# Decay blocks of a Mamba-2 branch: difference and bound moved from VectorE to 16 ScalarE activations a group, with two smaller moves

## The chip, the cores and the metric

The kernel runs on one core of a Trainium2 chip. The core has five engines that each work through their own list of instructions in order and wait for one another by semaphores: TensorE (PE, matrix products and transposes, with its weight loads shown apart as PEld), VectorE (DVE), ScalarE (ACT), GpSimd (POOL) and SyncE (SP, which here only starts DMA transfers). The metric is the device time of one execution in microseconds (us).

## The reference

Two layers, each a feed-forward block, a mixer and a second feed-forward block, on 256 positions of width 1024; a norm at the end. All arithmetic is float32. The mixer runs two branches side by side on the same normed input, a Mamba-2 state-space branch (SSD: 32 heads of 64 in 4 groups, chunks of 128 positions, so two chunks) and a gated DeltaNet branch (8 heads). The change lies in the SSD branch, in the matrix called `decay`:

```python
log_a = (dt * a).reshape(b, nc, L, G, hg)
a_cum = jnp.cumsum(log_a, axis=2)
causal = jnp.tril(jnp.ones((L, L), dtype=bool))[None, None, :, :, None, None]
seg = a_cum[:, :, :, None] - a_cum[:, :, None, :]
decay = jnp.where(causal, jnp.exp(jnp.where(causal, seg, 0.0)), 0.0)
cb = jnp.einsum("bclgn,bcsgn->bclsg", Cc, Bc)
y_diag = jnp.einsum("bclsg,bclsgh,bcsghp->bclghp", cb, decay, xdt)
```

For each head and chunk this is a 128x128 block: the exponential of the difference of two running sums, where the row is not before the column. `a` is negative, so the difference is at most zero there; where the row is before the column it may be positive, and the kernel bounds it at zero and lets the product with a masked `cb` make it zero.

## The kernel before

**Products in three parts.** A float32 product is made of three products of rounded halves: each operand is split into a high part (`...h`, `whi`) and a low one (`...l`, `wlo`), and high x high, high x low and low x high are summed in one bank of PSUM (`mm3`). Nearly all of TensorE's work is such products.

**Weights.** They come as tiles of 128x1024 from memory, started by SyncE into a ring of five buffers (`wraw`). `prep` splits a tile: ScalarE copies it to `whi` (line 68) and VectorE subtracts to get `wlo` (line 71), in rings of five each. `take` hands the next tile to the products and prepares those that follow. So each tile costs ScalarE one copy and VectorE one subtraction, whatever else these engines do, and when either falls behind by five tiles, TensorE stands.

**The mixer's order.** A table of step names (`ORDER`) says in which order the steps of the two branches are written; the scheduler then sets the order of each engine's list from the dependences, its own estimates, and priorities. The steps around the change, in their order in time:

- `ssd_pre` (lines 1038 to 1054): for each of 4 groups two products of B and C into a bank of PSUM (`cbb`); VectorE masks them into `cbm` and ScalarE copies the part across chunks into `cbx` (both shown as `cbt`). Banks come from two pools of four, `trb` (short-lived) and `accb` (accumulators).
- `decay(g)` (lines 1059 to 1074) for group g: a DMA spreads the running sums of the group's 8 heads over all partitions (`dc`, 128x2048: 8 heads, 2 chunks, 128 positions); VectorE subtracts the column `ac` (2048 wide in one instruction) and bounds at zero; ScalarE takes the exponential; VectorE multiplies by `cbm`. Two buffers, one for groups 0 and 2 and one for 1 and 3.
- `xs_unit(g, i)`: two weight tiles through TensorE (`xs`) give 256 channels of the SSD's input; ScalarE makes the first product of a convolution of four taps (`ca<-xs,lp`), VectorE the other three (`ca<-xs,lp,ca`, of 255, 254 and 253 positions), and ScalarE applies silu into `xsT`. Exp and silu are in different tables of ScalarE, so the lists have an `ACT_TABLE_LOAD` before the first of each.
- `ssd(g)`: TensorE turns `xsT` (`xsb`, 8 transposes); VectorE makes `xD`, `xdt`, `xe`; TensorE multiplies by the decay block (`ydb`) and by the carried state (`yob`); VectorE adds them into `xD` and multiplies by the gate (`yz`); ScalarE squares and sums (`jk`), VectorE scales the sums (`sss`), GpSimd takes the power -1/2 (`srr`, line 210), and ScalarE scales `yz` by it (`yz<-yz,srr`).
- `gate`: tanh of two more tiles of columns (`t`, `tg`).
- `dn_T(hp)` and the DeltaNet branch's projection: TensorE turns a pair of heads (`oT`), VectorE gates it (`og`), ScalarE makes its high part (`bh`), VectorE its low part (`bl`), and TensorE multiplies both with a weight tile into four accumulators (`b`, lines 335 to 337). The SSD branch's projection follows later in the same way from `yz` (`yT`).
- at the mixer's end the gated sum of both is turned (`mT`) and split into `mh` (ScalarE) and `ml` (VectorE), and `close` multiplies it with the output weights (`o`): the first two tiles as one group, in `out_chunks`, for positions 0 to 127 (t = 0) and then 128 to 255.

Work of several steps is under way at once: while the SSD heads of group g run, the inputs of group g + 1 and the decay of group g + 2 are made.

Of the kernel before, what the change touches and what calls it, by code (L numbers as in the profile page):

```python
# [10 lines left out]
AF = mybir.ActivationFunctionType  # L11
ALU = mybir.AluOpType
# [4 lines left out]
P = 128  # L17
# [7 lines left out]
GS = 4  # L25
# [28 lines left out]
def trunk_kernel(ctx, tc, x, wst, wsm, norms, lpar, rpar, cst, out):  # L54
    nc = tc.nc
    V, A, G, PE = nc.vector, nc.scalar, nc.gpsimd, nc.tensor
# [10 lines left out]
    def act(o, i, func=AF.Copy, **kw):  # L67
        return A.activation(out=o, in_=i, func=func, **kw)  # L68

    def tt(o, a, b, op):  # L70
        return V.tensor_tensor(out=o, in0=a, in1=b, op=op)  # L71
# [4 lines left out]
    def ts(o, a, s1, op0, sc2=None, op1=None):  # L76
        if op1 is None:
            return V.tensor_scalar(out=o, in0=a, scalar1=s1, scalar2=None, op0=op0)
        return V.tensor_scalar(out=o, in0=a, scalar1=s1, scalar2=sc2, op0=op0, op1=op1)
# [7 lines left out]
    def trb(name):  # L87
        return trp.tile([P, 512], F32, tag="tr", name=name)

    def accb(name):  # L90
        return accp.tile([P, 512], F32, tag="acc", name=name)

    def small(shape, name, bufs=2):
        return sm.tile(shape, F32, tag=name, name=name, bufs=bufs)
# [54 lines left out]
    state = {"loaded": 0, "prepped": 0, "taken": 0, "last": None, "hold": False, "behind": {}, "late": {}, "first": 0, "turns": {}, "first_chunk": False, "cap": n_forms}  # L149
# [52 lines left out]
    def take():  # L202
        j = state["taken"]
        state["taken"] = j + 1
        ahead("loaded", limit[min(j + NSPL, n_forms) - 1], load)
        ahead("prepped", min(j + 1 if state["hold"] else j + NSPL, n_forms, state["cap"]), prep)
        return halves.pop(j)
# [11 lines left out]
    h = cpool.tile([P, 2, D], F32, name="h")  # L219
# [114 lines left out]
    def mm3(ps, lh, ll, rh, rl, start, stop):  # L334
        PE.matmul(ps, lh, rh, start=start, stop=False)  # L335
        PE.matmul(ps, lh, rl, start=False, stop=False)  # L336
        return PE.matmul(ps, ll, rh, start=False, stop=stop)  # L337
# [55 lines left out]
                        cut and a == 0 and kt == 1,  # L393
                    )

    def out_chunks(ps, stat, ks, last, group=1, split=False, first=None):

        for g0 in range(0, len(ks), group):
            kk = ks[g0 : g0 + group]
            ws = [(k, take()) for k in kk]  # L400
            for t in range(2):
                order = [(k, n) for n in range(2) for k in range(len(kk))]
                if t == 1 and not split:
                    m = len(kk) - 2 if len(kk) == NSPL else len(kk)
                    order = [(k, n) for k in range(m) for n in range(2)]
                    order += [(k, n) for n in range(2) for k in range(m, len(kk))]
                order = [(k, n, 0, 512) for k, n in order]
                if t == 1 and split:
                    order = [o for o in order if o[1] == 0]
                    order += [(k, 1, c, c + 256) for c in (0, 256) for k in range(len(kk))]  # L410
                state["sums"] = []
                for k, n, c0, c1 in order:
                    k, (wh, wl) = ws[k]
                    sh, sl = stat(k, t)
                    c = slice(n * 512 + c0, n * 512 + c1)
                    begin = k == 0 if first is None else first and t == n == 1
                    bank = ps[t][n][:, c0:c1]
                    if c0:
                        begin, bank = k == kk[0], ps[2][:, 0:256]
                    ins = mm3(bank, sh, sl, wh[:, c], wl[:, c], begin, k == last)  # L420
                    state["sums"].append(ins)

    def residual(po, nw):
        def add(t):
            banks = [(po[t][n][:], n * 512) for n in range(2)]
            if nw is None and t == 1:
                banks.append((po[2][:, 0:256], 768))
            for bank, c0 in banks:
                hv = h[:, t, c0 : c0 + bank.shape[-1]]
                ins = stt(hv, bank, 0.5, hv, ALU.mult, ALU.add)  # L430
            return ins

        if nw is None:
            return add
        norm_in(nw, add)

    def close(po, stat, n_k, nw):

        out_chunks(po, stat, list(range(2)), n_k - 1, group=2)
        out_chunks(po, stat, list(range(2, n_k - NSPL)), n_k - 1)  # L440
        state["hold"] = True
        out_chunks(po, stat, list(range(n_k - NSPL, n_k)), n_k - 1, group=NSPL, split=nw is None)
        return residual(po, nw)
# [149 lines left out]
    def mixer(l, nxt):  # L593
# [50 lines left out]
        ac = small([P, 2, 40], "ac", 1)  # L644
# [393 lines left out]
        def ssd_pre():  # L1038
            BT, CT = late["BC"][:, 0:4], late["BC"][:, 4:8]
            cbt = slots.tile([P, 3 * GS, P], F32, tag="sF", name="cbt")  # L1040
            late["cbx"] = cbx = cbt[:, 2 * GS :]
            late["cbm"] = cbm = cbt[:, : 2 * GS].rearrange("p (g t) l -> p g t l", g=GS)
            for g in range(GS):
                cbb = trb("cbb")
                PE.matmul(cbb[:, 0 : 2 * P], BT[:, g, 0:P], CT[:, g, :], start=True, stop=True)
                PE.matmul(cbb[:, 2 * P : 3 * P], BT[:, g, P : 2 * P], CT[:, g, P : 2 * P], start=True, stop=True)
                tt(
                    cbm[:, g],
                    cbb[:].rearrange("p (t o l) -> p t o l", t=2, o=2)[:, :, 0, :],
                    U[:, None, :].to_broadcast([P, 2, P]),  # L1050
                    ALU.mult,
                )
                act(cbx[:, g], cbb[:, P : 2 * P])
            yield
# [4 lines left out]
        def decay(g):  # L1059
            dc = slots.tile([P, 8, 2, P], F32, tag=("sA", "sB")[g % 2], name="dc")  # L1060
            nc.sync.dma_start(
                dc[:].rearrange("p h t l -> p (h t l)"),
                rdram[8 * g : 8 * g + 8].rearrange("a b -> (a b)").partition_broadcast(P),
            )
            tt(
                dc[:], dc[:],
                ac[:, :, 8 * g : 8 * g + 8].rearrange("p t h -> p h t")[:, :, :, None].to_broadcast([P, 8, 2, P]),
                ALU.subtract,
            )
            dv = dc[:].rearrange("p h t l -> p (h t l)")  # L1070
            ts(dv, dv, 0.0, ALU.min)
            act(dv, dv, AF.Exp)
            tt(dc[:], dc[:], late["cbm"][:, g, None].to_broadcast([P, 8, 2, P]), ALU.mult)
            decs[g] = dc

# [102 lines left out]
        def branch(kind, n, mk, tail=1):  # L1178
            ps = [[accb("b"), accb("b")] for _ in range(2)]
            held = {}  # L1180

            def stat(k, t):
                oh, ol = held[k // 2]
                return oh[:, k % 2, t * P : (t + 1) * P], ol[:, k % 2, t * P : (t + 1) * P]

            made = 1
            for j0 in list(range(n - tail)) + [n - tail]:
                js = range(j0, j0 + (tail if j0 == n - tail else 1))
                while made < min(js[-1] + 2, n):
                    mk(made)  # L1190
                    made += 1
                for j in js:
                    held[j] = brT.pop((kind, j))
                out_chunks(ps, stat, [2 * j + i for j in js for i in range(2)], 2 * n - 1, group=2 * len(js))
            return ps
# [57 lines left out]
        ps = branch("s", 8, ss_T)  # L1253
# [20 lines left out]
        po = [[accb("o"), accb("o")] for _ in range(2)]  # L1274

        def stat(k, t):
            return mh[:, k, t * P : (t + 1) * P], ml[:, k, t * P : (t + 1) * P]

        close(po, stat, 8, nxt)

    norm_first(nw0)
# [157 lines left out]
```

## Time and profile before

| | us |
|---|---|
| median of 3 runs | 1544.98 |
| lowest and highest of them | 1544.69, 1545.77 |
| the profiled execution | 1543.84 |
| its span in the trace | 1542.1 |
| granted clock of TensorE, mean | 0.999 |

The profile comes from one execution; its times are those of the trace, counted from the start of the span. Rows of groups give count, busy time, mean duration and the idle time of the engine just before them with what ended it. Rows of the timeline give start, duration, engine, line, operation, out<-in, shapes, a count where like instructions follow one another, and in brackets the idle time before and its releaser. All activations share line 68, VectorE's two-operand operations line 71, and its three-operand ones line 74, so rows are told apart by their tiles. The names are those of the program without numbers. What belongs to the mixers lies, in the first layer, between about 300 and 600 us, and in the second 762 us later.

### The profile page before, as it was taken

How to read it: one execution, taken by the hardware profiler on the slowest of the kernel's cores; microseconds unless marked ns; L12 is line 12 of the kernel's file. 1: busy time of each engine (PE TensorE's matmuls, PEld its weight loads, DVE VectorE, ACT ScalarE, POOL GpSimd, SP SyncE). 2: the span in 40 equal slices, each digit the busy share in tenths (PEclk: the TensorE clock that was granted, in tenths of full speed). 3: DMA queues.
4: the chain of work that ended last, by engine and by line, in shares of the span. 5: the costliest groups of instructions: out<-in, count | busy, mean ns of one | idle time of the engine just before them, and what ended most of it. 6: DMA issues, size and time to landing. Idle time of an engine off the chain costs nothing.

```text
span 1542.1 us, 29082 instructions
## 1 busy us (share of the span) xinstructions
PE 1525.1 (99%) x11473; PEld 1385.3 (90%) x11473; DVE 1229.8 (80%) x1859; ACT 949.8 (62%) x1536; POOL 82.6 (5%) x92
## 2 busy tenths in 40 slices
PE   8999999999999999999999999999999999999998
PEld 7999879999988888999899998899998888899997
DVE  5878768967899766789778887689579996678886
ACT  5656667766665645566555566776756666455565
POOL 0000010000000000000100012010000000000010
PEclk9999999999999999999999999999999999999999
DMA  7687765553565556577866687566346555556775
GB/s 272 187 266 227 232 223 174 183 164 112 180 209 172 157 174 191 184 252 217 264 221 227 204 254 238 182 196 186 117 137 204 180 167 187 175 179 191 250 241 156
DMA packets 98831, 305.73 MB, mean 198 GB/s; under 512 B 22837, under 2 KB 23813, under 8 KB 97670
## 3 DMA queue, kind: packets, MB, share of 16 engines
q1 hardware_dynamic: 93796, 290.95, 57.1%
q0 software_dynamic: 4608, 12.58, 5.0%
q8 instruction: 90, 1.47, 0.4%
q14 instruction: 47, 0.39, 0.1%
q10 hardware_dynamic: 290, 0.33, 0.1%
HBM read 297.72 MB, written 1.92 MB: 194 GB/s over the span
## 4 chain that ended last, share of the span: by engine, by line
PE 90%; DVE 3%; ACT 3%; DMA 2%; issue 1%; POOL 0%; SPq 0%; POOLq 0%; ACTq 0%; DVEq 0%
PE fc L346 10%; PE fc L340 9%; PE fc L345 9%; PE t L366 9%; PE o L337 4%; PE o L336 4%; PE o L335 4%; PE f L366 3%; PE b L337 3%; PE b L335 3%; PE b L336 3%; PE p L336 2%; PE p L335 2%; PE p L337 2%; PE xs L340 1%; PE xs L345 1%
## 5 line engine op out<-in xcount | busy, mean ns | idle before, releaser
L71 DVE TENSOR_TENSOR wlo<-wraw,whi 128x1024 fp32r<-128x1024 f32 x488 | 592.2, 1222 | 189.9 <-ACT whi L68 175.4
L68 ACT ACTIVATE whi<-wraw 128x1024 fp32r<-128x1024 f32 x488 | 511.4, 1059 | 266.8 <-PE fc L345 87.3
L346 PE MATMUL fc<-uW,wlo 128*128 128x256 f32 x1280 | 354.9, 277 | 0.0
L340 PE MATMUL fc<-uW,whi 128*128 128x256 f32 x1280 | 354.1, 277 | 0.0
L345 PE MATMUL fc<-uW,whi 128*128 128x256 f32 x1260 | 348.3, 276 | 0.0
L340 PEld LDWEIGHTS fc<-uW,whi 128*128 128x128 f32 x1280 | 240.5, 188 | 0.8
L346 PEld LDWEIGHTS fc<-uW,wlo 128*128 128x128 f32 x1280 | 240.5, 188 | 0.0
L345 PEld LDWEIGHTS fc<-uW,whi 128*128 128x128 f32 x1260 | 236.5, 188 | 0.8
L366 PE MATMUL t<-whi,uW 128*128 128x512 f32 x512 | 165.4, 397 | 0.0
L366 PEld LDWEIGHTS t<-whi,uW 128*128 128x128 f32 x512 | 95.9, 188 | 21.6 <-issue 1.3
L68 ACT ACTIVATE whi<-wsum 128x1024 fp32r<-128x1024 f32 x64 | 68.0, 1062 | 58.7 <-PE fc L345 32.3
L366 PE MATMUL t<-wlo,uW 128*128 128x512 f32 x256 | 100.1, 392 | 0.0
L71 DVE TENSOR_TENSOR wlo<-wsum,whi 128x1024 fp32r<-128x1024 f32 x64 | 78.2, 1222 | 8.3 <-ACT whi L68 5.9
L335 PE MATMUL b<-whi,bh 128*128 128x512 f32 x192 | 76.1, 398 | 0.3 <-ACT bh L68 0.2
L336 PE MATMUL b<-wlo,bh 128*128 128x512 f32 x192 | 75.0, 390 | 0.0
L337 PE MATMUL b<-whi,bl 128*128 128x512 f32 x192 | 74.3, 394 | 0.3 <-DVE bl L71 0.3
L340 PE MATMUL xs<-uW,whi 128*128 128x256 f32 x256 | 72.8, 284 | 0.0
L346 PE MATMUL xs<-uW,wlo 128*128 128x256 f32 x256 | 71.4, 279 | 0.0
L345 PE MATMUL xs<-uW,whi 128*128 128x256 f32 x254 | 70.5, 278 | 0.0
L335 PE MATMUL o<-whi,gh 128*128 128x512 f32 (+1 forms) x160 | 62.0, 388 | 0.0
L337 PE MATMUL o<-whi,gl 128*128 128x512 f32 (+1 forms) x160 | 61.8, 386 | 0.0
L336 PE MATMUL o<-wlo,gh 128*128 128x512 f32 (+1 forms) x160 | 61.7, 386 | 0.0
(337 smaller groups left out, 3301.2 us busy)
## 6 DMA issues: line engine op xcount, KB each, us to landing
wraw<-in_wst_dram SPq DMA_DIRECT2D x504, 512.0 KB, 4.8
wsum<-in_wst_dram SPq DMA_DIRECT2D x16, 512.0 KB, 7.3
wsum<-in_wst_dram POOLq DMA_DIRECT2D x16, 512.0 KB, 8.6
dc<-rdram SPq DMA_DIRECT2D x8, 1024.0 KB, 8.6
nw<-in_norms_dram SPq DMA_DIRECT2D x6, 512.0 KB, 5.3
h<-u POOLq DMA_DIRECT2D x12, 256.0 KB, 6.4
gb<-rdram SPq DMA_DIRECT2D x8, 256.0 KB, 6.1
h<-in_x_dram SPq DMA_DIRECT2D x4, 256.0 KB, 3.7
```

Source lines behind the costliest of these rows:

```text
L68: return A.activation(out=o, in_=i, func=func, **kw)
L71: return V.tensor_tensor(out=o, in0=a, in1=b, op=op)
L335: PE.matmul(ps, lh, rh, start=start, stop=False)
L336: PE.matmul(ps, lh, rl, start=False, stop=False)
L337: return PE.matmul(ps, ll, rh, start=False, stop=stop)
L340: PE.matmul(ps, wh, mh, start=start, stop=False)
L345: PE.matmul(ps, wh, ml, start=False, stop=False)
L346: PE.matmul(ps, wl, mh, start=False, stop=stop)
L366: ins = PE.matmul(ps[t][:], st, mv, start=k0 == 0 and j == 0, stop=k0 == KT - 2 and j == 5)
```

## The change

Three edits. In `decay`, the two VectorE instructions are replaced by 16 ScalarE activations of 128x128, one for each head and chunk: Relu with scale -1 and the column of `ac` as bias, that is max(ac - dc, 0), and the exponential then has scale -1. The product with `cbm` stays. In `ssd_pre`, the fourth group's bank comes from the accumulators' pool. In `close`, the first group's low x high products for t = 0 are issued after its other products.

```diff
-    def out_chunks(ps, stat, ks, last, group=1, split=False, first=None):
+    def out_chunks(ps, stat, ks, last, group=1, split=False, first=None, defer=False):
...
-                state["sums"] = []
+                state["sums"], lows = [], []
                 for k, n, c0, c1 in order:
                     k, (wh, wl) = ws[k]
                     sh, sl = stat(k, t)
...
+                    if defer and t == 0:
+                        PE.matmul(bank, sh, wh[:, c], start=begin, stop=False)
+                        PE.matmul(bank, sh, wl[:, c], start=False, stop=False)
+                        lows.append((bank, sl, wh[:, c]))
+                        continue
                     ins = mm3(bank, sh, sl, wh[:, c], wl[:, c], begin, k == last)
                     state["sums"].append(ins)
+                for bank, sl, high in lows:
+                    PE.matmul(bank, sl, high, start=False, stop=False)
...
-        out_chunks(po, stat, list(range(2)), n_k - 1, group=2)
+        out_chunks(po, stat, list(range(2)), n_k - 1, group=2, defer=True)
...
-                cbb = trb("cbb")
+                cbb = trb("cbb") if g < GS - 1 else accb("cbb")
...
-            tt(
-                dc[:], dc[:],
-                ac[:, :, 8 * g : 8 * g + 8].rearrange("p t h -> p h t")[:, :, :, None].to_broadcast([P, 8, 2, P]),
-                ALU.subtract,
-            )
             dv = dc[:].rearrange("p h t l -> p (h t l)")
-            ts(dv, dv, 0.0, ALU.min)
-            act(dv, dv, AF.Exp)
+            for hh in range(8):
+                for t in range(2):
+                    act(dc[:, hh, t], dc[:, hh, t], AF.Relu, scale=-1.0, bias=ac[:, t, 8 * g + hh : 8 * g + hh + 1])
+            act(dv, dv, AF.Exp, scale=-1.0)
             tt(dc[:], dc[:], late["cbm"][:, g, None].to_broadcast([P, 8, 2, P]), ALU.mult)
             decs[g] = dc
```

The scheduler gives other lists around these edits, in both layers alike; outside the stretch from `cbb` to the output projection the lists do not change. Three places follow.

ScalarE, from DeltaNet's last chunk to the second Exp of the decay blocks (`dc<-dc 128x2048` is the Exp, `dc<-dc,ac` are the new activations). Before:

```order
L68 ACTIVATE o_4924<-vb 128x512
L68 ACTIVATE cbt<-cbb 128x128 x4
L68 ACTIVATE whi<-wraw 128x1024
L68 ACT_TABLE_LOAD
L68 ACTIVATE dc<-dc 128x2048
L68 ACTIVATE whi<-wraw 128x1024
L68 ACTIVATE tg<-t_4953 128x512
L68 ACTIVATE whi<-wraw 128x1024
L68 ACTIVATE dc<-dc 128x2048
```

and with the change, from the table load to the second Exp (16 of group 0 and the first of group 1 stand ahead of it, among o and the four cbt):

```order
L68 ACTIVATE dc<-dc,ac 128x128 x6
L68 ACT_TABLE_LOAD
L68 ACTIVATE dc<-dc 128x2048
L68 ACTIVATE whi<-wraw 128x1024 x2
L68 ACTIVATE tg<-t_4953 128x512
L68 ACTIVATE dc<-dc,ac 128x128 x2
L68 ACTIVATE whi<-wraw 128x1024
L68 ACTIVATE dc<-dc,ac 128x128
L68 ACTIVATE tg<-t_4954 128x512
L68 ACTIVATE whi<-wraw 128x1024
L68 ACTIVATE dc<-dc,ac 128x128 x12
L68 ACTIVATE dc<-dc 128x2048
```

Ahead of the second Exp there are now 32 activations more, and four weight copies where there were three.

VectorE, at the SSD heads of group 1, where the decay block of group 2 is made. Before (its product, `dc<-dc,cbt`, follows only later, after `og`):

```order
L71 TENSOR_TENSOR xe<-xdt,dE 128x512
L78 TENSOR_SCALAR dc<-dc 128x2048
L71 TENSOR_TENSOR wlo<-wraw,whi 128x1024
L74 SCALAR_TENSOR_TENSOR ca<-xs,lp,ca 128x255
L71 TENSOR_TENSOR xD<-xD,ydb 128x512
L74 SCALAR_TENSOR_TENSOR ca<-xs,lp,ca 128x254
```

and with the change:

```order
L71 TENSOR_TENSOR xe<-xdt,dE 128x512
L71 TENSOR_TENSOR wlo<-wraw,whi 128x1024
L71 TENSOR_TENSOR dc<-dc,cbt 128x2048
L71 TENSOR_TENSOR wlo<-wraw,whi 128x1024
L74 SCALAR_TENSOR_TENSOR ca<-xs,lp,ca 128x255
L71 TENSOR_TENSOR xD<-xD,ydb 128x512
L74 SCALAR_TENSOR_TENSOR ca<-xs,lp,ca 128x254
```

The product, which needs the third Exp, has moved up to where the bound at zero stood, ahead of a weight tile's low part, the convolution's adds and the heads' sums. One group earlier it is the same: there it had stood behind all of these.

ScalarE, at the start of DeltaNet's projection. Before:

```order
L68 ACTIVATE jk,sss<-yz 128x512
L68 ACTIVATE whi<-wraw 128x1024
L68 ACTIVATE jk,sss<-yz 128x512
L68 ACTIVATE ca<-xs,lp 128x256
L68 ACTIVATE bh<-og 128x512
L68 ACTIVATE xsT<-ca 128x256
L68 ACTIVATE yz<-yz,srr 128x512 x2
```

and with the change:

```order
L68 ACTIVATE jk,sss<-yz 128x512
L68 ACTIVATE whi<-wraw 128x1024
L68 ACTIVATE xsT<-ca 128x256
L68 ACTIVATE yz<-yz,srr 128x512 x2
L68 ACTIVATE bh<-og 128x512
L68 ACTIVATE dc<-dc,ac 128x128 x9
L68 ACTIVATE bh<-og 128x512
```

The high part of the first pair of heads (`bh`) now stands behind the two scalings that wait for GpSimd's `srr`, and 9 of group 3's activations stand between it and the next.

TensorE has the same products. One pair of `cbb` moved ahead of the gate's `t`; the 8 transposes `xsb` of group 1 are in one piece (before, the last two came after 15 products); the 12 transposes `oT` and the first four `yT` stand ahead of the DeltaNet branch's products (before, two and four of them came among these). SyncE issues group 2's load of `dc` one weight tile earlier.

## The prediction, made before the changed kernel was run

> **What bounds the kernel now.** The page of the profiled execution was read first: busy shares, then the chain that ended last.
>
> ```profile
> PE 1525.1 (99%) x11473; PEld 1385.3 (90%) x11473; DVE 1229.8 (80%) x1859; ACT 949.8 (62%) x1536; POOL 82.6 (5%) x92
> PE 90%; DVE 3%; ACT 3%; DMA 2%; issue 1%; POOL 0%; SPq 0%; POOLq 0%; ACTq 0%; DVEq 0%
> ```
>
> TensorE (PE) is busy 1525.1 us of a span of 1542.1: work taken off another engine gains only where PE waits for it, and work put on one costs only where PE begins to wait. So the view of PE's waits comes second; these are the rows near the change:
>
> ```profile
> PE xsb L1101 <- ACT xsT L68: 1.7, 2, 0.9
> PE cbb L1045 <- DVE vb L71: 1.3, 2, 0.9
> PE o L337 <- DVE ml L71: 0.6, 2, 0.3
> PE b L337 <- DVE bl L71: 0.3, 1, 0.3
> PE b L335 <- ACT bh L68: 0.2, 1, 0.2
> ```
>
> Together 4.1 us over both layers: all that this change can win. Third, the stretch from the first decay block to the end of the DeltaNet branch in layer 1 (us, then busy time of PE, PEld, DVE, ACT, POOL), and the decay blocks' own operations (ns):
>
> ```profile
> 403.00:484.00 81.00, 79.12 (x571) 68.42 (x571) 77.21 (x100) 51.47 (x71) 4.81 (x3) 1.00 0.53 176
> L71 DVE TENSOR_TENSOR dc<-dc,ac x8: 2280/2284/2293, 403.4 to 1233.8; 128x2048 f32<-128x2048 f32 x8
> L78 DVE TENSOR_SCALAR dc<-dc x8: 1218/1220/1223, 409.8 to 1251.2; 128x2048 f32<-128x2048 f32 x8
> L68 ACT ACTIVATE dc<-dc x8: 1901/1918/1924, 412.4 to 1254.7; 128x2048 f32<-128x2048 f32 x8
> L71 DVE TENSOR_TENSOR dc<-dc,cbt x8: 2280/2285/2293, 415.4 to 1256.6; 128x2048 f32<-128x2048 f32 x8
> ```
>
> VectorE is busy 77.2 of 81 us here and ScalarE 51.5. Layer 2 repeats it 762 us later with the same order, so the sum is worked for layer 1 and doubled.
>
> **What the parts cost.** Times below are from one start to the next on an engine, which is shorter than a duration, because neighbours overlap. ScalarE's rows (groups by shape, then the timeline):
>
> ```profile
> L68 ACT ACT_TABLE_LOAD x30 | 38.5, 1283 | 18.6 <-DVE ca L74 16.5 <-PEq L1428 1.7
> L68 ACT ACTIVATE ca<-xs,lp 128x256 f32<-128x256 f32 x32 | 17.4, 549 | 0.0
> L68 ACT ACTIVATE xsT<-ca 128x256 f32<-128x256 f32 x32 | 13.0, 411 | 20.8 <-DVE ca L74 20.8
> L68 ACT ACTIVATE kd<-turned,dT 128x128 f32<-128x128 f32 x24 | 7.7, 412 | 0.0
> L68 ACT ACTIVATE bsc<-sf 128x128 fp32r<-128x128 f32 x16 | 4.8, 300 | 1.0 <-DVE sf L71 1.0
> L68 ACT ACTIVATE cbt<-cbb 128x128 f32<-128x128 f32 x8 | 2.0, 271 | 1.8 <-DVE cbt L71 1.5
> ...
> 394.70 1.15 ACT L68 ACTIVATE os<-qsb,eG 128x128 f32<-128x128 f32 x4 [0.51 <-PE qsb L954]
> 406.84 0.43 ACT L68 ACTIVATE cbt<-cbb 128x128 f32<-128x128 f32 x2
> 416.62 1.90 ACT L68 ACTIVATE dc<-dc 128x2048 f32<-128x2048 f32 x1
> 418.43 0.59 ACT L68 ACTIVATE tg<-t 128x512 f32<-128x512 f32 x1
> 428.26 1.28 ACT L68 ACT_TABLE_LOAD   x1 [3.56 <-DVE ca L74]
> 457.11 0.62 ACT L68 ACTIVATE jk<-yz 128x512 f32<-128x512 f32 x1
> 459.91 0.62 ACT L68 ACTIVATE bh<-og 128x512 fp32r<-128x512 f32 x1
> 462.16 1.34 ACT L68 ACTIVATE yz<-yz,srr 128x512 f32<-128x512 f32 x2 [1.32 <-POOL srr L210]
> 472.68 4.85 ACT L68 ACTIVATE whi<-wraw 128x1024 fp32r<-128x1024 f32 x5
> ```
>
> An overlap of about 0.1 us (Exp 1.90, the next start 1.81 later) makes Exp 1.82, whi 0.96, table load 1.29, xsT 0.32, ca 0.45, tg 0.48, bh 0.52, and jk (with its read of the sum) and one yz 0.62 each.
>
> The new operation, a 128x128 activation from SBUF with a per-partition column, is not in this trace. Nearest: four os in 1.15 us, with a column but from PSUM, are 0.26 apart ((1.15 - 0.37)/3); a source in SBUF lengthens bsc (300 ns) over cbt (271) by 0.03. I take **0.29**. Lower end 0.17: the second of two cbt, without a column (0.43 - 0.26). Upper end 0.41: kd, with a column and no overlap. By the Trainium skill ("ScalarE: Activation LUTs", What ACT_TABLE_LOAD costs) a column adds about 93 ns, so the operation would last 387 ns, and 294 if the neighbours overlap; no run here yet shows whether they do with a bias.
>
> *Decay.* Per group VectorE loses the subtract (2.20 between starts) and the min (1.14), 3.34 us; ScalarE gains 16 x 0.29 = 4.64 us. That VectorE is the fuller engine would speak for it. But the work lies in a chain (difference, Exp, product), and both engines run in order, so I follow the chain. VectorE's and GpSimd's rows for it:
>
> ```profile
> 403.38 2.29 DVE L71 TENSOR_TENSOR dc<-dc,ac 128x2048 f32<-128x2048 f32 x1 [0.64 <-DMA dc<-rdram]
> 415.39 2.29 DVE L71 TENSOR_TENSOR dc<-dc,cbt 128x2048 f32<-128x2048 f32 x1
> 417.60 2.36 DVE L71 TENSOR_TENSOR wlo<-wraw,whi 128x1024 fp32r<-128x1024 f32 x2
> 426.12 0.68 DVE L71 TENSOR_TENSOR xD<-xD,ydb 128x512 f32<-128x512 f32 x1
> 426.72 0.48 DVE L74 SCALAR_TENSOR_TENSOR ca<-xs,lp,ca 128x254 f32<-128x254 f32 x1
> 458.64 0.74 DVE L74 SCALAR_TENSOR_TENSOR og<-oT,lp,zdT 128x512 f32<-128x512 f32 x1
> ...
> 432.73 1.60 POOL L210 TENSOR_TENSOR srr<-sss,mhalf 128x2 f32<-128x2 f32 x1 [23.59 <-DVE sss L79]
> 459.92 2.21 POOL L210 TENSOR_TENSOR srr<-sss,mhalf 128x2 f32<-128x2 f32 x1 [25.59 <-DVE sss L79]
> ```
>
> Product 2.20, wlo 1.14, xD, yo and yz 0.60 each, ca 0.40, og 0.66.
>
> *Station 1.* Group 0's rows land at 403.4. From there to the end of the second Exp, ScalarE has 32 bias activations 9.28, o 0.52, four cbt 0.68, a table load 1.29, two Exp 3.64, four whi 3.84, two tg 0.96: 20.2, so 423.6. Before, that Exp ended at 416.62 + 1.90 = 418.5.
>
> *Station 2.* VectorE's product of group 1 now stands ahead of the conv's adds and xD, and holds them until 423.6. Then product 2.20, wlo 1.14, three adds 1.20, two xD 1.20: the third add ends at 429.4. ScalarE's table load behind Exp waits for that add (before: the load began at 428.26), so the 5 us are mostly swallowed by a wait of 3.56 that was there already.
>
> *Station 3.* From 429.4: table load 1.29, four xsT 1.28, three ca 1.35, two jk 1.24, six whi 5.76, two yz 1.24, two tg 0.96, group 2's 16 activations 4.64, table load 1.29, Exp 1.82, and 1.05 of waiting for GpSimd's first srr: third Exp ends at 451.4. Ten of the 16, with table load and Exp, stand behind group 1's last xsT, which so comes at 444.0.
>
> ```profile
> 442.56 0.82 PE L1101 MATMUL xsb<-cs,xsT 128*128 128x128 f32 x6
> 446.04 0.44 PE L1101 MATMUL xsb<-cs,xsT 128*128 128x128 f32 x2 [0.93 <-ACT xsT L68]
> ```
>
> PE took six of the eight transposes at 442.56 and waited 0.93 for the last two; now all eight stand in the first place, which PE, without its waits ahead of that (0.46 at cbb and smaller ones), reaches at 441.6. It waits 2.5 there.
>
> *Station 4.* VectorE stands at group 2's product until 451.4, with wlo, the conv's adds and xD of group 1 behind it: 5.74 as in station 2, 457.2; then yo, yz, xD, wlo, add, yz 3.94, 461.2; add, og, add 1.46, and sss at 462.7 (before 459.9). GpSimd's srr 2.2: 465.0. ScalarE's yz x2, which wait for it, 1.24: 466.3. **bh, which stood ahead of yz x2, now stands behind it**: 0.52, 466.8. PE begins the branch at 466.9.
>
> ```profile
> 460.58 0.50 PE L335 MATMUL b<-whi,bh 128*128 128x512 f32 x1 [0.17 <-ACT bh L68]
> 483.94 1.04 PE L1101 MATMUL xsb<-cs,xsT 128*128 128x128 f32 x8
> ```
>
> That is 6.3 later than 460.58. The branch before took 23.4 us (to 483.94), of it two oT and four yT transposes and the waits at bl. The transposes now stand ahead of it, and 96 products at 0.228 are 21.9; but ScalarE copies no weight tile for some 13 us around bh, group 3's 16 activations and its Exp, and five prepared tiles at 24 products x 0.228 / 2 = 2.7 us each last just as long: 0.95 of waiting for the next whi. So 22.8 instead of 23.4, and the branch ends 5.7 later. Group 3's product has room: its own xsb follow only then.
>
> *Bank for cbb.* The fourth pair no longer waits for a bank that vb's reader holds (0.4 in layer 1, 0.9 in layer 2 by the waits' row). The gain lies ahead of station 1, where PE is early anyhow: nothing, and without the decay's delay at most 1.3 in all.
>
> *Late low products.* They use ml, for which PE waited 0.3 in each layer; behind the first half's high products it has been made: -0.6 in all. The same products, the same count.
>
> *SyncE.* Group 2's load is issued one weight load earlier; its buffer is free and nothing waits on the order: 0 to 0.3.
>
> **Sum.** 2 x 5.7 - 0.6 = +10.8 on the profiled execution of 1543.84 us, which is 1.14 under the runs' median of 1544.98: about **1555.7** for the median.
>
> **Rivals.**
>
> *Faster.* All 4.1 us of waits go: 1544.98 - 4.1 = 1540.9. The place is station 1: only if the second Exp ends by 418.5 as before does VectorE profit from 3.34 us less a group. That needs 32 activations within 15.1 - 10.9 = 4.2 us, 0.13 each. For it: VectorE is the fuller engine. Against it: even the cheapest row gives 0.17, and bh would still stand behind yz x2.
>
> *No change.* At 0.17 the 48 activations ahead of the third Exp shrink by 5.8, but then VectorE's own work holds the chain: sss comes at 459.2, yz x2 and bh still follow srr, PE starts at 463.4. That is 2.8 late, less the 1.5 by which the branch is shorter than 23.4: +1.3 a layer, 1547.0. Up to 0.20 or so this is within 0.2% (3 us, about what can be told from no change).
>
> *Worse.* At 0.41 without overlap 32 activations end the second Exp at 427.5 instead of 423.6, the third at 457.0 instead of 451.4 (48 x 0.12), PE starts at 472.4, and the weight copies behind group 3's activations come 2.1 late instead of 0.95: +13.2 a layer, 1570.8. Speaking for it: kd. Against it: os, which overlaps with a column too.
>
> *The change does not do what it says:* a Relu that calls for another table. The order has the same number of table loads as before, so I give this no share of its own.
>
> The Trainium skill ("ScalarE: Activation LUTs", Rules for kernel authors) says to put relu, min and add on VectorE, not ScalarE; by it the change can only lose, and the rows agree as far as 3.34 us against 4.64 go.
>
> **Chances and range.** Forecast (late bh and starved copies, 1549 to 1564) 0.73; worse 0.10; no change 0.10; faster 0.07. Between 0.20 and 0.35 per activation the end moves from +1.6 to +9.5 a layer, 1547.6 to 1563.4; the range 1547 to 1564 leaves out about 0.2. Faster by over 0.2% 0.07, within it 0.10, slower 0.83.
>
> **What would show it.** Right: bias activations about 0.29 apart; the second and third Exp of layer 1 ending near 423.6 and 451.4; VectorE idle ahead of the products for ACT dc; PE waiting 2 to 3 us each at xsb and at the branch's first b for ACT; the waits at cbb and o gone. Wrong: an activation pitch under 0.20, the product not at the head of VectorE's queue when Exp ends, a wait of PE somewhere in the SSD heads or the ssm branch that I do not have, or weights arriving late.

## The result, and the profile after

The change costs 11.6 us: 1556.6 us against 1545.0 (medians of five runs each), a ratio of 1.0081 [1.0070, 1.0092]. 1555.7 was predicted, with a range of 1547 to 1564. The profiled execution spans 1554.3 us, 12.2 more than the one before.

The page of the kernel after, busy time of each engine and the engines' shares of the chain that ended last:

```profile
PE 1528.0 (98%) x11473; PEld 1388.2 (89%) x11473; DVE 1205.3 (78%) x1843; ACT 984.1 (63%) x1664; POOL 78.2 (5%) x92
PE 88%; ACT 6%; DVE 2%; DMA 2%; issue 1%; POOL 0%; SPq 0%; POOLq 0%; ACTq 0%; DVEq 0%
```

VectorE lost 24.5 us of work, ScalarE gained 34.3, and ScalarE's share of the chain doubled from 3 to 6%. Next, PE's waits after (us in all, times, longest):

```profile
PE b L335 <- ACT bh L68: 6.7, 2, 3.4
PE yT L1173 <- DVE og L74: 3.4, 2, 1.9
PE xsb L1105 <- ACT xsT L68: 2.2, 2, 1.1
```

The waits at `cbb` and for `ml` are gone, as meant. In their place PE waits once in each layer 3.4 us for `bh` and 1.5 to 1.9 for the `og` ahead of it. Stretches after (us, then busy time of PE, PEld, DVE, ACT, POOL, granted clock, DMA share, GB/s):

```profile
403.00:484.00 81.00, 74.61 (x542) 64.82 (x541) 63.89 (x89) 71.03 (x138) 3.31 (x3) 0.96 0.49 167
...
468.00:474.00 6.00, 6.00 (x15) 4.66 (x16) 4.95 (x10) 6.00 (x19) 0.00 (x0) 0.51 0.31 97
474.00:480.00 6.00, 6.00 (x28) 4.95 (x27) 3.08 (x3) 5.94 (x7) 0.00 (x0) 1.00 0.00 0
```

Neither engine is full in the stretch of 81 us: VectorE is busy 63.9, ScalarE 71.0, and still PE stands idle 6.4 us where it stood 1.9. This looks like waiting in order, not lack of an engine; experiment 9 tests it. The second thing was not foreseen: from 468 to 474 TensorE's granted clock is 0.51, and PE gets through 15 products where the same six microseconds later hold 28.

Where the time arises, by PE's timeline (start us, us, instruction, idle time before it). Before:

```profile
400.34 1.05 PE L973 MATMUL vnb<-rh,TT 128*128 128x128 f32 x8
1162.21 1.05 PE L973 MATMUL vnb<-rh,TT 128*128 128x128 f32 x8
1223.18 0.50 PE L335 MATMUL b<-whi,bh 128*128 128x512 f32 x1
1245.83 1.04 PE L1101 MATMUL xsb<-cs,xsT 128*128 128x128 f32 x8
```

and after:

```profile
402.07 1.05 PE L980 MATMUL vnb<-rh,TT 128*128 128x128 f32 x8
445.33 0.66 PE L1105 MATMUL xsb<-cs,xsT 128*128 128x128 f32 x4 [1.15 <-ACT xsT L68]
...
467.75 0.79 PE L335 MATMUL b<-whi,bh 128*128 128x512 f32 x1 [3.37 <-ACT bh L68]
468.34 0.63 PE L336 MATMUL b<-wlo,bh 128*128 128x512 f32 x1
468.77 0.63 PE L335 MATMUL b<-whi,bh 128*128 128x512 f32 x1
492.50 1.03 PE L1105 MATMUL xsb<-cs,xsT 128*128 128x128 f32 x8
...
1169.21 1.05 PE L980 MATMUL vnb<-rh,TT 128*128 128x128 f32 x8
1234.79 0.62 PE L335 MATMUL b<-whi,bh 128*128 128x512 f32 x1 [3.37 <-ACT bh L68]
1258.28 1.03 PE L1105 MATMUL xsb<-cs,xsT 128*128 128x128 f32 x8
```

`vnb` stands ahead of all that was changed and is late already: by 1.73 in layer 1 (the two executions differ before it: PE waits 1.4 us at `pst` after and 0.5 before, for one) and by 7.00 in layer 2 (layer 1 left 8.56, of which 1.56 were made up in between). Less that lag, the branch's first product is 5.4 late in layer 1 (467.75 - 460.58 - 1.73) and 4.6 in layer 2; the branch's end, at `xsb` of group 2, is 6.8 and 5.5 late. Together 12.3, where the spans differ by 12.2; the 1.73 from ahead of the change and what was made up outside the two stretches nearly cancel. The time is lost where the prediction put it.

### The profile page after: what moved, and what is told of

Its sections match the earlier page's. It is cut to its first block, busy times and chain, and to the rows that moved or that the text cites. A ratio compares the mean times of both kernels' runs of the same rounds, so it can differ in the third digit from the quotient of the medians.

```text
span 1554.3 us, 29196 instructions
## 1 busy us (share of the span) xinstructions
PE 1528.0 (98%) x11473; PEld 1388.2 (89%) x11473; DVE 1205.3 (78%) x1843; ACT 984.1 (63%) x1664; POOL 78.2 (5%) x92
## 4 chain that ended last, share of the span: by engine, by line
PE 88%; ACT 6%; DVE 2%; DMA 2%; issue 1%; POOL 0%; SPq 0%; POOLq 0%; ACTq 0%; DVEq 0%
PE fc L346 9%; PE fc L340 9%; PE fc L345 9%; PE t L366 8%; PE o L336 4%; PE o L337 4%; PE o L335 4%; PE f L366 3%; PE b L335 3%; PE b L336 3%; PE b L337 3%; ACT dc L68 2%; PE p L336 2%; PE p L337 2%; PE p L335 2%
```

## The experiments

Ratios are against the kernel before, run beside it on the same chip; the experiments ran on several chips, so they are compared with one another by their ratios (0.001 is 1.5 us) rather than by medians. Theory A and rival B are what each recorded text calls so. "The change" is the kernel after.

**1. Which edit is it?** The decay edit alone, the bank and the late low products undone:

```diff
-                cbb = trb("cbb") if g < GS - 1 else accb("cbb")
+                cbb = trb("cbb")
...
-        out_chunks(po, stat, list(range(2)), n_k - 1, group=2, defer=True)
+        out_chunks(po, stat, list(range(2)), n_k - 1, group=2)
```

> Only the decay edit; the bank for cbb and the low products as before. Theory A (the decay edit alone makes the kernel slower, the two small edits win at most what PE waited at ml): 1556.6 + 0.6 = 1557.2 us, between 1556 and 1559, with PE's wait for bh at the DeltaNet branch's first b of about 3.4 us in each layer as with the whole change. Rival B (the early fourth bank, which fills an accumulator's bank just ahead of the branch, is part of the loss): at least 2 us less than the whole change, under 1554.5.

Measured: 1557.5, ratio 1.0084 [1.0070, 1.0097], the waits for `bh` and `og` as in the change. A is right: the decay edit alone carries the loss.

**2. The small edits without the decay edit.** Subtract, min and a plain Exp as before; bank and late low products kept:

```diff
-            for hh in range(8):
-                for t in range(2):
-                    act(dc[:, hh, t], dc[:, hh, t], AF.Relu, scale=-1.0, bias=ac[:, t, 8 * g + hh : 8 * g + hh + 1])
-            act(dv, dv, AF.Exp, scale=-1.0)
+            tt(
+                dc[:], dc[:],
+                ac[:, :, 8 * g : 8 * g + 8].rearrange("p t h -> p h t")[:, :, :, None].to_broadcast([P, 8, 2, P]),
+                ALU.subtract,
+            )
+            ts(dv, dv, 0.0, ALU.min)
+            act(dv, dv, AF.Exp)
```

> Decay as before; only the bank for cbb and the low products put last. Theory A: PE's waits at cbb (1.3 us in both layers) and at ml (0.6) go, others stay: 1544.97 - 1.9 = 1543.1 us, between 1542 and 1545. Rival B (the small edits cost something, or the waits only move to xsb and to the branch): 1545 to 1547.

Measured: 1548.0, ratio 1.0015 [1.0005, 1.0025]. The gain of up to 1.9 us is not there; B is right, and the cost is a little over what it allowed. The waits, the timeline and a window of this run:

```profile
PE xsb L1108 <- ACT xsT L68: 4.2, 2, 2.2
```

```profile
447.81 0.44 PE L1108 MATMUL xsb<-cs,xsT 128*128 128x128 f32 x2 [2.03 <-ACT xsT L68]
```

```profile
448.00:450.00 2.00, 2.00 (x13) 2.00 (x13) 2.00 (x4) 0.00 (x0) 0.00 (x0) 0.60 0.86 272
```

The waits at `cbb` went, and the one at `xsb` grew from 1.7 to 4.2, and behind a wait of 2.03 the granted clock was 0.60 in the two microseconds shown and 0.54 in the next two. Less the 1.05 by which this execution was late beforehand, PE comes to these transposes 0.5 sooner than before (442.07 against 442.56), and group 1's last `xsT` begins 0.7 later (446.29 against 445.57). VectorE's list differs there: group 1's product now stands ahead of the second `yz` of group 0. That this is the reason was not tested.

**3. The late low products alone.** Experiment 2 with the bank undone as well:

```diff
-                cbb = trb("cbb") if g < GS - 1 else accb("cbb")
+                cbb = trb("cbb")
```

> Only the low products put last; decay and bank as before. The lists differ from before only around the output projection. Theory A (the 2 us that e2_bank_and_low loses come from the bank, which moves the scheduler's order up to the xsb of group 1; the low products win the 0.6 us at ml): 0.6 under the kernel before of the same chip, about 1545.4, which these runs can hardly tell from no change. Rival B (the low products last cost the 2 us): 1547 to 1548.

Measured: 1545.2, ratio 1.0001 [0.9992, 1.0010]. The 0.6 us that were priced can't be told from nothing. So the 2 us of experiment 2 go with the bank: the two ratios differ by 0.0014, just more than both intervals together leave to chance.

**4. `bh` ahead of `yz`.** The change, with the first scalings of the branch's input put ahead in the scheduler's order:

```diff
+            with tc.high_priority(offset=PRI):
-            act(oh[:].rearrange("p a t -> p (a t)"), og[:])
-            tt(ol[:].rearrange("p a t -> p (a t)"), og[:], f(oh[:]).rearrange("p a t -> p (a t)"), ALU.subtract)
+                act(oh[:].rearrange("p a t -> p (a t)"), og[:])
+                tt(ol[:].rearrange("p a t -> p (a t)"), og[:], f(oh[:]).rearrange("p a t -> p (a t)"), ALU.subtract)
```

> The whole change, with the high and low parts of the DeltaNet heads at a higher priority, so that the first bh stands ahead of the two yz that wait for GpSimd; ScalarE's and VectorE's work is the same. Theory A (bh behind yz is what the first b waits for, and the clock falls during that wait): the first b starts 3.4 us sooner, at full clock, which gives another 2.8 us in layer 1 and 1.6 in layer 2; then the weight copies behind group 3's activations are late by about 3 us in each layer, which gives back half: about 1551.5 us, between 1548 and 1553.5. Rival B (the order of bh does not matter, the products held up on VectorE do): at most 1 us gained, over 1555.5.

Measured: 1551.4, ratio 1.0038 [1.0026, 1.0051]: half of the loss is gone. Its timeline:

```profile
465.75 0.62 ACT L68 ACTIVATE bh<-og 128x512 fp32r<-128x512 f32 x1
467.79 1.34 ACT L68 ACTIVATE yz<-yz,srr 128x512 f32<-128x512 f32 x2 [1.12 <-POOL srr L210]
466.42 0.50 PE L335 MATMUL b<-whi,bh 128*128 128x512 f32 x1 [0.70 <-ACT bh L68]
```

`bh` no longer stands behind `yz`, PE waits 0.70 instead of 3.37, and the clock stays at 1.00 through layer 1's branch (in layer 2 the wait of 1.88 for `og` and one of 0.7 for `bh` close behind it still bring it to 0.50). A is right. Place and cause of about half the loss are so shown: `bh` queued behind two instructions that wait for GpSimd (the priority holds for the later pairs and for `bl` as well). Two effects go together in it, the wait and the half clock behind it.

**5. Is the half clock worth something by itself?** The change, with products into an unused bank ahead of the branch, so that PE does not stand still while it waits for `bh`:

```diff
+FILL = 13
...
+            for _ in range(FILL if j == 0 else 0):
+                PE.matmul(bank[:], uTh[:, 0, 0:P], uTh[:, 0:2, :], start=True, stop=True)
```

> The whole change, with 12 idle products of 128x512 (0.23 us each, 2.8 us) on PE between the head transposes and the first b of the DeltaNet branch, in a bank that is overwritten afterwards; the output is the same. Theory A (the clock falls to half because PE stands idle for over 3 us, and costs 2.8 us in layer 1 and 1.6 in layer 2, less some 0.9 in each layer for the weight copies that then come late): 1556.6 - 4.4 + 1.8 = 1554 us, between 1552.5 and 1555.3, and the granted clock at 1.00 throughout the branch. Rival B (the slow products have another cause than PE's idling): clock 0.5 there as well, 1556 to 1558.5.

Measured: 1553.3, ratio 1.0054 [1.0042, 1.0067], 3.3 us under the change by the medians and 4.2 by the ratios (0.0027 x 1545), with 26 products more (13 a layer, 12 of them in the row below). Timeline and windows:

```profile
463.54 4.61 PE L1171 MATMUL yT<-uW 128*128 128x512 f32 x12 [1.87 <-DVE og L75]
```

```profile
464.00:467.00 3.00, 3.00 (x9) 2.34 (x8) 2.60 (x3) 1.96 (x5) 1.60 (x1) 0.50 0.39 105
467.00:470.00 3.00, 3.00 (x13) 2.45 (x13) 2.13 (x4) 3.00 (x11) 0.00 (x0) 0.93 0.83 269
```

The wait of 1.87 for `og` by itself brings the clock to 0.50; the half clock then falls on the filling products, and the branch itself starts at full clock. `bh` comes no earlier than in the change, so what is gained is the clock's part. In the profiled execution the branch lasts 22.45 and 22.55 us in the two layers, 3.2 less than in the change together, but begins 1.2 and 0.7 later. So A is right, and the 4.5 us worked out below for the clock are won back for the most part.

**6. The product of the decay block behind the work that it held up.** The change, with groups 1 and 2's products issued only after the last gated `yz`; the scheduler then puts `bh` ahead of `yz` without the priority of 4:

```diff
+        def product(g):
+            with ExitStack() as behind:
+                if g in (1, 2):
+                    behind.enter_context(tc.issue_after(state["gated"].ins))
+                tt(dc[:], dc[:], late["cbm"][:, g, None].to_broadcast([P, 8, 2, P]), ALU.mult)
```

> The whole change, with the products of groups 1 and 2 on VectorE held back until the gated sums (yz) of the group before are made; ScalarE has the same instructions, and the scheduler then puts bh ahead of yz by itself. Theory A (what costs is VectorE standing at the products for ScalarE's Exp, with the conv's adds and the heads' sums behind them): against e3_bh_first (1551.4), which differs from it only by the products' place, another 2 to 5 us: 1546 to 1549.5 us, PE's waits at xsb under 1 us. Rival B (ScalarE's 4.64 us more a group are what costs, wherever the product stands): 1550.5 or more.

Measured: 1550.9, ratio 1.0038 [1.0024, 1.0052]; A's 1546 to 1549.5 is missed, and the time is B's. The timeline:

```profile
433.49 2.28 DVE L71 TENSOR_TENSOR dc<-dc,cbt 128x2048 f32<-128x2048 f32 x1
446.56 0.44 PE L1112 MATMUL xsb<-cs,xsT 128*128 128x128 f32 x2 [1.94 <-ACT xsT L68]
```

VectorE no longer waits at that product, but nine of group 2's activations (six in the change) now stand ahead of group 1's last `xsT`, and PE waits 1.94 there, with 3.4 us of half clock behind it, and the same in layer 2. A wait was not removed but moved, from VectorE's queue into ScalarE's. Experiment 9 tells whether B is right all the same.

**7. Half the activations.** Four of eight heads as activations, four with a subtract and a max on VectorE:

```diff
-            for hh in range(8):
+            for hh in range(4):
...
+            dh = dc[:, 4:]
+            tt(
+                dh, ac[:, :, 8 * g + 4 : 8 * g + 8].rearrange("p t h -> p h t")[:, :, :, None].to_broadcast([P, 4, 2, P]),
+                dh, ALU.subtract,
+            )
+            dh = dv[:, 4 * 2 * P :]
+            ts(dh, dh, 0.0, ALU.max)
```

> The whole change, but only heads 0 to 3 of each group on ScalarE (8 activations a group); the other four get a subtract and a bound of 1024 columns on VectorE. Theory A (the loss begins where the second and third Exp end so late that VectorE stands at the products; with 16 activations ahead of the second Exp in place of 32 it ends before VectorE gets there): less than a third of the loss, under 1549.8 us, and no idle time of VectorE ahead of the products of groups 1 and 2. Rival B (the loss goes with the number of activations): half of it, about 1551.3.

Measured: 1556.9, ratio 1.0080 [1.0068, 1.0093]: both missed. Half the new work, the same loss. PE's waits (and 4.5 at `xsb`) and ScalarE's timeline:

```profile
PE b L335 <- ACT bh L68: 8.5, 2, 4.3
```

```profile
444.88 1.92 ACT L68 ACTIVATE dc<-dc 128x2048 f32<-128x2048 f32 x1
...
448.11 0.42 ACT L68 ACTIVATE xsT<-ca 128x256 f32<-128x256 f32 x1
```

Group 2's Exp with its table loads now comes out ahead of group 1's last `xsT`, and `bh` still follows `yz`. So the loss does not go with the amount of work put on ScalarE, as the prediction's sum, activation by activation, has it.

**8. The same fusion on VectorE.** The difference and the bound as one two-step operation per head and tile, 16 a group:

```diff
-                    act(dc[:, hh, t], dc[:, hh, t], AF.Relu, scale=-1.0, bias=ac[:, t, 8 * g + hh : 8 * g + hh + 1])
-            act(dv, dv, AF.Exp, scale=-1.0)
+                    ts(dc[:, hh, t], dc[:, hh, t], ac[:, t, 8 * g + hh : 8 * g + hh + 1], ALU.subtract, 0.0, ALU.min)
+            act(dv, dv, AF.Exp)
```

> Bank and low products as in the change, but the difference and the bound both on VectorE, as 16 tensor_scalar of 128x128 a group with two operations each (subtract the column, then min with zero), instead of one subtract and one min of 128x2048. Theory A (freed time on VectorE, which is the fuller engine here, shortens the chain by itself, if no work goes to ScalarE): 16 of them at an estimated 0.14 to 0.17 us, from the min's 1.14 us for 2048 columns (0.07 for 128) and the 0.09 to 0.10 that a narrow VectorE row costs beside its columns, are 2.2 to 2.7 us a group against 3.34: 1541 to 1545.5 us, faster than before. Rival B (VectorE's load is not what sets the end, or a small instruction costs over 0.21): 1546 to 1549, like e2_bank_and_low.

Measured: 1548.7, ratio 1.0023 [1.0013, 1.0033]. The group (ns, min/median/max) and the longest run of them:

```profile
L79 DVE TENSOR_SCALAR dc<-dc,ac x128: 271/278/288, 403.5 to 1254.1; 128x128 f32<-128x128 f32 x128
```

```profile
408.34 3.22 DVE L79 TENSOR_SCALAR dc<-dc,ac 128x128 f32<-128x128 f32 x16
```

They are (3.22 - 0.28)/15 = 0.196 apart, so 16 take 3.14 where one subtract and one min took 3.34: hardly anything gained, and PE waits 6.4 for `bh` as well. B is right.

**9. The order set by hand, all 128 activations kept.** As 6, with the priority of 4 for `bh`, and group 2's activations issued only after the last `silu` of group 1's second convolution, group 3's behind the last `bh`, group 2's product behind the last `bl`:

```diff
+            with ExitStack() as behind:
+                if g > 1:
+                    behind.enter_context(tc.issue_after(state["turned" if g == 2 else "high"].ins))
...
+                if g in (1, 2):
+                    behind.enter_context(tc.issue_after(state["gated" if g == 1 else "low"].ins))
...
+            with tc.high_priority(offset=PRI):
+                state["high"] = act(oh[:].rearrange("p a t -> p (a t)"), og[:])
```

> The whole change with all its ScalarE activations, but their places set by hand: group 2's behind the last silu (xsT) of group 1, group 3's behind the last bh, bh ahead of the second yz, and VectorE's products of groups 1 and 2 behind the sums of the heads and behind the last bl. Theory A (the loss is PE's waits at xsb and at the first b and the half clock after each wait of about 2 us, and so the order, not ScalarE's 4.64 us more a group): no wait of PE over 1.5 us between 403 and 500 us, the granted clock at 1.00, and 1544 to 1548 us, within 3 us of the kernel before. Rival B (ScalarE's added work costs by itself, whichever its order): 1549.5 us or more, with PE waiting for whi or bh elsewhere.

Measured: 1542.2, ratio 0.9984 [0.9974, 0.9994]: faster than the kernel before by 2.5 us (the interval leaves 0.9 to 4), 14 us under the change, and better than A expected. PE's waits, layer 1's stretch (columns as above), and a piece of the timeline:

```profile
PE xsb L1117 <- ACT xsT L68: 1.8, 2, 1.1
PE b L335 <- ACT bh L68: 0.4, 1, 0.4
```

```profile
403.00:484.00 81.00, 80.22 (x579) 69.73 (x578) 67.56 (x94) 69.67 (x138) 3.30 (x3) 1.00 0.59 194
```

```profile
423.34 1.91 ACT L68 ACTIVATE dc<-dc 128x2048 f32<-128x2048 f32 x1
433.07 2.28 DVE L71 TENSOR_TENSOR dc<-dc,cbt 128x2048 f32<-128x2048 f32 x1
460.07 0.62 ACT L68 ACTIVATE bh<-og 128x512 fp32r<-128x512 f32 x1
460.90 1.32 ACT L68 ACTIVATE yz<-yz,srr 128x512 f32<-128x512 f32 x2
```

The second Exp ends at 425.25. Less the 1.18 by which this execution was late beforehand (`vnb` at 401.52), that is 424.1, as late as in the change and 5.6 later than before, and it costs nothing: no one waits for it now. ScalarE is as busy as in the change (69.7 against 71.0), `bh` is at its old place ahead of `yz`, and PE is idle 0.8 us in this stretch, where it was 1.9 before and 6.4 in the change.

**10. The same places, the old operations.** As 9, with subtract and min in place of the 16 activations (the diff of 2), so that the edit itself is compared with the order held:

```diff
-                for hh in range(8):
-                    for t in range(2):
-                        act(dc[:, hh, t], dc[:, hh, t], AF.Relu, scale=-1.0, bias=ac[:, t, 8 * g + hh : 8 * g + hh + 1])
...
+                ts(dv, dv, 0.0, ALU.min)
```

> The places set by hand of e12_order_mended, but the decay's difference and bound on VectorE as in the kernel before; so it differs from e12_order_mended by what the change does to decay, and from e2_bank_and_low by the places. Theory A (what e12_order_mended wins comes from VectorE's 3.34 us a group, which are free once nothing of PE's waits for ScalarE): 1545 us or more, 3 or more over e12_order_mended. Rival B (it comes from the places set by hand, and the decay edit is worth nothing): 1541.5 to 1543.5.

Measured: 1546.9, ratio 1.0015 [1.0006, 1.0024]. Its stretch and its waits:

```profile
403.00:484.00 81.00, 78.25 (x564) 66.91 (x562) 77.84 (x97) 54.98 (x73) 4.82 (x3) 1.00 0.49 162
```

```profile
PE xsb L1120 <- ACT xsT L68: 2.4, 2, 1.3
PE b L335 <- DVE ca L74: 1.3, 2, 0.7
```

With VectorE at 77.8 of 81, PE waits for VectorE's `ca` at the branch. Against experiment 9 the ratio is 1.0015/0.9984 = 1.0031: with these places, the activations are worth 4.8 us (the two intervals leave 2.7 to 6.9). A is right. These places were made for the activations, so it does not say what subtract and min could reach in an order of their own; 11 tries a part of one.

**11. The other two kernels with parts of the order set by hand.** Experiment 8 with `bh` as in 4 and group 1's last convolution at high priority; and the kernel before with that priority alone:

```diff
+                with ExitStack() as sooner:
+                    if (g, i) == (1, 1):
+                        sooner.enter_context(tc.high_priority(offset=PRI))
```

> e7_fused16 with two priorities: bh and bl of the DeltaNet heads, and the convolution of group 1's last 256 channels (the xsT that xsb waits for). Theory A (e7_fused16 is slower than before through PE's 3.2 us at the first b in each layer and the half clock behind it, about 3 us in all of it beyond the waits): those go, 1541 to 1545 us. Rival B (the waits move to another place): 1546 to 1549.

> The kernel before with one priority, for the convolution of group 1's last 256 channels; nothing of the change. Theory A (PE's 1.7 us at xsb go, and nothing else moves): 1 to 2 us under the kernel before, 1543 to 1544.3 where before is 1545.0 to 1546.0. Rival B (the wait moves on to the first b, where bh has 0.2 us to spare): no change, 1544.5 to 1546.5.

Measured: 1550.3, ratio 1.0028 [1.0017, 1.0039], and 1545.4, ratio 1.0000 [0.9991, 1.0008]. PE's waits of the first:

```profile
PE b L335 <- ACT bh L68: 5.4, 4, 2.1
PE xsb L1108 <- ACT xsT L68: 2.6, 2, 1.8
```

Here the waits only changed places. In the kernel before, the wait of 1.7 at `xsb` is gone, and waits for `bh` of 2.0 in all have come: that priority gains it nothing. In both B is right, the first being 1 us over what B allowed.

## Why the prediction was right, and what it missed

ScalarE's, VectorE's and GpSimd's timeline after, which the next points are read from:

```profile
420.27 3.61 ACT L68 ACTIVATE dc<-dc,ac 128x128 f32<-128x128 f32 x12
423.92 1.91 ACT L68 ACTIVATE dc<-dc 128x2048 f32<-128x2048 f32 x1
...
450.95 1.91 ACT L68 ACTIVATE dc<-dc 128x2048 f32<-128x2048 f32 x1
452.89 2.29 DVE L71 TENSOR_TENSOR dc<-dc,cbt 128x2048 f32<-128x2048 f32 x1 [2.53 <-ACT dc L68]
...
463.96 0.17 DVE L79 TENSOR_SCALAR sss<-sss 128x2 f32<-128x2 f32 x1
464.21 1.60 POOL L210 TENSOR_TENSOR srr<-sss,mhalf 128x2 f32<-128x2 f32 x1 [25.86 <-DVE sss L79]
465.84 1.33 ACT L68 ACTIVATE yz<-yz,srr 128x512 f32<-128x512 f32 x2 [1.04 <-POOL srr L210]
467.08 0.61 ACT L68 ACTIVATE bh<-og 128x512 fp32r<-128x512 f32 x1
```

Measured times below are these less the 1.73 that layer 1 was late beforehand.

| step | predicted | measured |
|---|---|---|
| bias activations apart, us | 0.29 | (3.61 - 0.39)/11 = 0.293 |
| second Exp ends | 423.6 | 424.1 |
| third Exp ends | 451.4 | 451.1 |
| PE's wait at `xsb` | 2.5 | 1.15 |
| `sss` ends | 462.7 | 462.4 |
| `srr` takes | 2.2 | 1.60 |
| first product of the branch | 466.9 | 466.0 |
| length of the branch, layers 1 and 2 | 22.8 | 24.75, 23.49 |
| branch's end later by, layers 1 and 2 | 5.7 | 6.8, 5.5 |

- **Stations 1 to 4** held: the chain from the activations over Exp, VectorE's product and the convolution's adds to `sss` within 0.5 us, and on over `srr`, `yz` and `bh` to the branch within 0.9, of which `srr` makes 0.6. VectorE stands idle ahead of the product for ScalarE's Exp as forecast, 1.26 us for group 1 and 2.53 for group 2. `bh` behind `yz` is shown by experiment 4. The price of a new operation was right; its group after (ns, min/median/max):

```profile
L68 ACT ACTIVATE dc<-dc,ac x128: 385/391/403, 405.3 to 1240.8; 128x128 f32<-128x128 f32 x128
```

  The Trainium skill ("ScalarE: Activation LUTs", What ACT_TABLE_LOAD costs) gives about 280 ns and 0.833 for each of 128 columns, 387, and 93 of overlap between neighbours, so 294 from one to the next; the trace agrees, with 391 and 293.
- **`xsb`** was oversized: four of the eight transposes still went ahead, PE came there 0.2 later and `xsT` 0.4 earlier than predicted, so the wait is 1.15. PE's wait at the branch's first `b`, 3.37, is over the 2 to 3 forecast, and the 1.87 and 1.49 at `yT` are a wait that the prediction did not have, one of its own signs of being wrong.
- **The branch's length** was the mis-sized term, and for a wrong reason. The 0.95 of waiting for the next `whi` did not come. In its place came a term that the prediction does not have, although it expected waits of 2 to 3 us: PE ran at half clock behind its wait for `bh`: products 0.43 apart (468.34 to 468.77) instead of 0.228. The 96 products need 21.9, so 2.85 in layer 1 and 1.6 in layer 2 are the clock's, 4.5 together. The trace's own record of the clock agrees: 0.50 from 467.03 to 473.85 and from 1235.03 to 1238.44, of which 6.1 and 3.4 us lie in the branch, and half of these is 3.05 and 1.7. Experiment 5 got 3.3 to 4.2 of it back. The sum came out near because the branch began 0.9 to 1.7 us earlier than predicted and ran 0.7 to 2.0 longer: two errors that nearly cancel, which is luck.
- **The small edits** were priced at -0.6 together, which no run shows. The bank costs about 2 us when it stands without the decay edit (2 against 3); beside it that does not show (experiment 1 against the change: ratios of 1.0084 and 1.0081).
- **The rival "faster"** had too narrow a condition. It said that this needs the second Exp by 418.5, so 0.13 an activation. Experiment 9 is faster with 0.293 and with that Exp at 425.25 (424.1 less its lag). What must not be late is `xsT` and `bh`; the Exp may be, if the product that waits for it is not ahead of others in VectorE's queue.
- **The rival "worse"** is added up wrongly: a start of the branch 11.8 late and copies 2.1 late make +12.4 a layer, 1569.2, not +13.2 and 1570.8. And `kd` did not speak for it: its row, 24 of 412 ns in 7.7 us busy, shows an overlap too.

So the prediction foresaw the loss and its path rightly, but not what it depends on. Experiments 7, 9 and 10 show that the 4.64 us a group on ScalarE are not the price; the price is the order in which the scheduler set the new operations between old ones, and the half clock that PE's waits bring with them. The Trainium skill ("ScalarE: Activation LUTs", Rules for kernel authors) would put relu, min and add on VectorE; the change as written agrees, experiments 9 and 10 do not: where VectorE is busy 77 of 81 us and ScalarE 51, the activations win by 4.8 us once nothing waits behind them.

Left open: how the half of the loss that experiment 4 leaves is shared among the other waits; why the bank delays group 1's last `xsT`; and whether subtract and min gain as much in an order set for them.

## What to carry to other kernels

When work moves to the engine with more room, ask of each queue which short operation now stands behind a long or waiting one: here `bh` behind two `yz` cost about half of 11.6 us, while 34 us more of work on ScalarE cost nothing once the order was right. Before an edit is dropped because it lost, try it with the operations that others wait for put first, and compare the old operations in the same places. Price a wait of TensorE of about 2 us or more with the slow stretch that may follow it too.

## What the runs showed of the hardware

**The clock falls after shorter waits than expected, and on a fixed grid.** Every trace records the granted clock, 1.00 or 0.50, with its times. Away from the program's end a stretch at 0.50 lasted 3.41 or 6.83 us, and within a trace all the changes lie whole multiples of 3.413 us apart: in experiment 7 the half clock begins at 449.27, 469.75, 1217.27 and 1237.75, which is 6, 219 and 6 steps. Laid on this grid, TensorE's idle time parts the cases without exception in all 14 traces, from their first record (13 to 17 us into the span) on: behind each step at full clock with 1.87 us of idle time or more the clock fell (31 steps, 14 of them at the program's end), behind none with 1.84 or less (6227 steps). The full clock came back behind a step without idle time, and not behind ones with 0.72 and 1.62.

So it counts where a wait lies. The 1.87 us ahead of experiment 5's filling products lie in one step and brought the half clock. The 1.96 us at `xsb` in the same run are divided into 0.33 and 1.63 and did not, and in experiment 8 not even 3.20 us did, divided into 1.74 and 1.46:

```profile
1226.47 0.50 PE L335 MATMUL b<-whi,bh 128*128 128x512 f32 x1 [3.20 <-ACT bh L68]
```

```profile
1225.00:1232.00 7.00, 5.53 (x27) 4.51 (x28) 5.55 (x10) 4.83 (x8) 0.00 (x0) 1.00 0.22 75
```

The Trainium skill ("TensorE: Matmul & The Clock Gate", What's actually happening) gives half the clock after an idle window of about 3.4 us, with windows that run freely. The half rate, the length of 3.41 us and the free-running windows agree with these traces. A window need not be idle as a whole: 1.87 us of its 3.41 were enough here.

**Sixteen small operations on VectorE cost what two large ones do.** 128 columns with a column operand, both steps in one, take 278 ns and come 0.196 us apart; 16 of them, 3.14 us, are hardly cheaper than the two operations of 2048 columns, 3.34.
